# Seven block products for the last twelve weight chunks of a hybrid convolution and attention layer

## The chip, the cores and the metric

One core of a Trainium2 chip. The time is device microseconds of one launch. The engines are TensorE (PE, its weight loads PEld), VectorE (DVE), ScalarE (ACT), GpSimd (POOL, idle here) and SyncE (SP), whose queue issues nearly all transfers. Every engine takes its queue in order.

## What is computed

One layer over 512 tokens of width 1024 (and 256 context tokens), cut from the reference:

```python
h  = rmsnorm(x, pre_g) * (1 + sc) + sh              # sc, sh, gt = split(silu(c) @ w_mod + b_mod)
b_gate, c_gate, x_in, z_a, q, k, v, z_b, g_a, g_b = split(h @ w_in)      # ten blocks of 1024 columns
attn = neighbourhood_attention(rope(q), rope(k), v, k_ctx, v_ctx, rpb)   # 16 heads of 64
y_a = (silu(z_a) * b_gate * dwconv3(c_gate * x_in, conv_w, conv_b)) @ w_out_conv
y_b = (silu(z_b) * attn) @ w_out_attn
y   = (sigmoid(g_a) * y_a + sigmoid(g_b) * y_b) @ w_o
out = x + gt * rmsnorm(y, post_g)
```

All in fp32.

## The kernel before

**Products.** An fp32 operand is held as two fp32r tiles, H (a cast on ScalarE) and L (the remainder, a subtraction on VectorE); `split` (L67) makes both. A product is H·H + H·L + L·H, three matmuls for each 128 rows of depth. Activations stand with channels on the partitions and tokens along the free axis (`hx`, 8 tiles of 128 channels x 512 tokens).

**Weight chunks.** `w_in` and the two output projections are read in chunks of 1024 rows x 256 columns: two units of 128 columns. `Chunk` loads one as two raw halves of 512 KB (`raw`), and splits each half (128x1024 on ACT and on DVE) into a tile `w`. `Chunks` keeps one chunk ahead. `unit(w, i)` multiplies a unit with h: 24 matmuls of 512 columns (`step_T`, L115 to L117).

**Stages.** First x is normed, the modulation computed and the first three chunks multiplied, in an order written by hand (`manual_schedule`). Then four convolution groups and the modulated context; here `conv_out` (L191) writes its result to `u`, eight halves of four tiles in SBUF. Then attention: eight pairs of heads, for each head four blocks of 128 queries (64 score blocks in all): scores on PE, the addition of the bias with a minimum on DVE (L568), exp and scaling on ACT, transposes (L583) whose result is split into TH and TL, and the product with V (`gather`, L599). Between the blocks stand the chunks that `plan` names for each pair: queries and keys (`qk`), values (`v`), the later convolutions (`cx`, `bz`), gates of the attention (`zb`) and merge gates (`g`). The last gate `gate2(3)` follows, and the splits of u and attention into `us` and `as` (L696).

Then eight merges: `y_j` multiplies a chunk of output projections with `us` and `as`, is gated with `G[j]` and summed to the merged tile `m`; the merge gates g2 to g7 stand between y0 to y6, one after each. At last comes the product with `w_o`, which is done in seven block products already (L801).

The order within the stages that are not written by hand is the Tile framework's: its scheduler orders each engine's instructions by the data they need and by their place in the code, and pools' buffers decide which load can start.

Of the kernel before, what the change touches and what calls it, by code (L numbers as in the profile page):

```python
# [15 lines left out]
P = 128  # L16
D = 1024
# [10 lines left out]
def layer(ctx: ExitStack, tc, xp, ctxt, ctxT, cc, wmod, small, wfirst, win, wout, wo, rel, tab, out):  # L28
# [6 lines left out]
    pp = ctx.enter_context(tc.tile_pool(name="pp", bufs=1, space=bass.MemoryType.PSUM))  # L35

# [18 lines left out]
    def pairs(tag, n, dtype=F32R):  # L55
        t = [hp.tile([P, 2, n], dtype, name=f"{tag}{k}") for k in range(KT)]
        return t, ([x[:, 0] for x in t], [x[:, 1] for x in t])

    def halves(tag):
        t = [hp.tile([P, 2, S], F32, name=f"{tag}{i}") for i in range(4)]  # L60
        return [t[i // 2][:, i % 2] for i in range(KT)]


    _, hx = pairs("h", S)
    hcs, hc = pairs("hc", C)
# [11 lines left out]

    class Chunk:


        def __init__(self, src):
            self.raws = [wp.tile([P, 4, 256], F32, name="raw", bufs=2) for _ in range(2)]
            for i, raw in enumerate(self.raws):
                nc.sync.dma_start(raw, src[:, 4 * i:4 * i + 4])

        def split(self):
            both = wp.tile([P, KT, 2, 256], F32R, name="w", bufs=2)
            for i, raw in enumerate(self.raws):
                s = slice(4 * i, 4 * i + 4)
                split(both[:, s, 0], both[:, s, 1], raw)  # L90
            return both[:, :, 0], both[:, :, 1], both

    def load_chunk(src):
        return Chunk(src).split()

    class Chunks:
# [5 lines left out]
        def load(self, n):  # L102
            if n < len(self.srcs) and n not in self.ahead:
                self.ahead[n] = load_chunk(self.srcs[n])

        def __call__(self):
            self.load(self.n)
            self.n += 1
            self.load(self.n)
            return self.ahead[self.n - 1]  # L110

    def step_T(ps, w, u, m, k):
        (H, L, _), (mH, mL) = w, m
        cs = slice(u * P, (u + 1) * P)
        nc.tensor.matmul(ps, lhsT=H[:, k, cs], rhs=mH[k], start=k == 0, stop=False)  # L115
        nc.tensor.matmul(ps, lhsT=H[:, k, cs], rhs=mL[k], start=False, stop=False)  # L116
        nc.tensor.matmul(ps, lhsT=L[:, k, cs], rhs=mH[k], start=False, stop=k == KT - 1)  # L117
# [6 lines left out]
    def proj_N(ps, w, m, ts):  # L124

        (H, _, both), (mH, mL) = w, m
        for k in range(KT):
            nc.tensor.matmul(  # L128
                ps, lhsT=mH[k][:, ts], rhs=both[:, k].rearrange("p a c -> p (a c)"), start=k == 0, stop=False,
                skip_group_check=True,  # L130
            )
        for k in range(KT):
            nc.tensor.matmul(  # L133
                ps[:, :256], lhsT=mL[k][:, ts], rhs=H[:, k], start=False, stop=k == KT - 1, skip_group_check=True
            )

    def proj_c(ps, w, u):

        (H, L, _), cs = w, slice(u * P, (u + 1) * P)
        for k in range(KT):  # L140
            nc.tensor.matmul(  # L141
                ps, lhsT=H[:, k, cs], rhs=hcs[k].rearrange("p a c -> p (a c)"), start=k == 0, stop=False,
                skip_group_check=True,
            )
        for k in range(KT):
            nc.tensor.matmul(  # L146
                ps[:, :C], lhsT=L[:, k, cs], rhs=hc[0][k], start=False, stop=k == KT - 1, skip_group_check=True
            )
# [29 lines left out]
    order = [win[i] for i in range(8)] + [qk(0), vz(0, 0)]  # L178
    order += [where[n](i) for f in plan for n, i in f] + [vz(3, 1)]
    for j in range(KT):  # L180
        order += [wout[j]] + ([win[34 + j]] if j < 6 else [])
# [53 lines left out]
    with ExitStack() as p0:  # L235
# [36 lines left out]
        ones = const.tile([1, P], F32, name="ones")  # L272
# [6 lines left out]
        u = halves("u")  # L279
# [35 lines left out]
        with tc.manual_schedule(engines={E.PE, E.DVE, E.Activation, E.SP}):  # L315
# [74 lines left out]
            for k in range(KT):  # L390
# [15 lines left out]
                elif k == 5:  # L406
                    after = Chunk(order[3])
# [62 lines left out]
    attn = halves("a")  # L470
# [137 lines left out]
    def gate(p, w, i):  # L608
        psz = unit(w, i)
# [7 lines left out]
    def gate2(g):  # L617
        w = chunk()
        gate(2 * g, w, 0)
        yield  # L620
        gate(2 * g + 1, w, 1)
        yield
# [3 lines left out]
    def merge_gates(j):  # L626
        w = chunk()
        G[j] = []
        for i in range(2):
            n = 2 * j + i  # L630
            g = hp.tile([P, S], F32, name=f"g{n}", tag=f"hc{n % 8}")
            nc.scalar.activation(g, unit(w, i), AF.Tanh, scale=0.5)  # L632
            G[j].append(g)
            yield
# [13 lines left out]
    convs = {j: conv(j) for j in range(4, KT)}  # L648
# [53 lines left out]
    raws = [hp.tile([P, 2, S], F32, name=f"m{i}", tag=f"u{i}") for i in range(4)]  # L702
    m2 = [raws[i // 2][:, i % 2] for i in range(KT)]
# [7 lines left out]
    def block(name, pool, tags):  # L711
# [19 lines left out]
    A11, S3 = operand("A11", hp, ("a0", "a1")), operand("S3", hp, ("a2", "a3"))  # L731
    B11, B12 = block("B11", bp, ("B0", "B1")), block("B12", bp, ("B2", "B3"))
# [10 lines left out]
    for j in range(KT):  # L743
        w = chunk()
        g = G[j]
        for i in range(2):
# [3 lines left out]
            if j == 7 and i == 0:  # L750
                A2 = [bp.tile([P, 2, S], F32R, name=f"A2{k}", tag=f"us{k}") for k in range(4)]
                for k in range(3):
                    split(A2[k][:, 0], A2[k][:, 1], m2[k + 4])
        nc.vector.tensor_add(m2[j], g[0], g[1])
        if j < 4:
            split(A11[j // 2][:, 0, j % 2], A11[j // 2][:, 1, j % 2], m2[j][:, h0])
        if j == 1 or j == 3:
            q = j // 2
            x = cv.tile([P, S], F32, name="tb").rearrange("p (k c) -> p k c", k=2)
            nc.vector.tensor_sub(x, raws[q][:, :, h0], raws[q][:, :, h1])  # L760
            split(S3[q][:, 0], S3[q][:, 1], x)
        if j < 6:
            for _ in merge_gates(j + 2):
                pass
        if j == 3:
            load_block(B11, 0, 0)
            load_block(B12, 0, 1)
        if j == 4:
# [4 lines left out]
            for i in range(2):  # L773
# [6 lines left out]
                nc.scalar.copy(gpost[:, i * S:(i + 1) * S], ps)  # L780
        if j == 5:
            sums1(0)
            B22, B21, T2, T3 = (block(n, hp, (f"h{2 * i}", f"h{2 * i + 1}")) for i, n in enumerate(("B22", "B21", "T2", "T3")))
            load_block(B22, 1, 1)
            load_block(B21, 1, 0)
        if j == 6:
            nc.scalar.activation(const.tile([P, 1], F32, name="dummy2"), G[7][1][:, :1], AF.Sqrt, bias=eps, scale=0.0)
# [8 lines left out]
    def product(ps, a, w, start, t, cols=slice(0, S), out=None):  # L796
# [9 lines left out]
    def both(ps, a, w, start, then=lambda t: None):  # L806
        for t in range(2):
            product(ps[t], a, w, start, t)
            then(t)

    xr = [[hp.tile([P, S], F32, name=f"xr{t}{i}", tag=f"hc{2 * t + i}") for i in range(2)] for t in range(4)]
# [25 lines left out]
    def close(t, n, parts):  # L837
# [157 lines left out]
```

## Time and profile before

| | |
|---|---|
| median of 3 runs | 723.36 us (723.33 to 723.99) |
| the profiled execution's own time | 723.86 us |
| its span, first to last instruction | 722.1 us |
| granted TensorE clock | 0.999 |
| busy: PE, DVE, ACT | 711.1, 507.3, 392.8 us |
| read and written in HBM | 83.93 MB, 2.10 MB |

The profile is of the profiled execution, which is 0.5 us above the median. In the page's rows an operation stands by its line in the kernel, its engine, and its tiles, written out<-in. A line can be that of a helper: nearly all splits have the lines of `split` (L70 on ACT, L71 on DVE), so there the tile tells what it is. Matmuls overlap each other in their records; what one costs in a row of them is the distance of their starts.

### The profile page before, as it was taken

How to read it: one execution, taken by the hardware profiler on the slowest of the kernel's cores; microseconds unless marked ns; L12 is line 12 of the kernel's file. 1: busy time of each engine (PE TensorE's matmuls, PEld its weight loads, DVE VectorE, ACT ScalarE, POOL GpSimd, SP SyncE). 2: the span in 40 equal slices, each digit the busy share in tenths (PEclk: the TensorE clock that was granted, in tenths of full speed). 3: DMA queues.
4: the chain of work that ended last, by engine and by line, in shares of the span. 5: the costliest groups of instructions: out<-in, count | busy, mean ns of one | idle time of the engine just before them, and what ended most of it. 6: DMA issues, size and time to landing. Idle time of an engine off the chain costs nothing.

```text
span 722.1 us, 9274 instructions
## 1 busy us (share of the span) xinstructions
PE 711.1 (98%) x3476; PEld 596.9 (83%) x3476; DVE 507.3 (70%) x955; ACT 392.8 (54%) x706; POOL 0.7 (0%) x6
## 2 busy tenths in 40 slices
PE   7999999999999999999999999999999999999996
PEld 4888888888888888888888888888888888888885
DVE  6979999794887848758768678565763333343997
ACT  6576533674676755755657647555742223133573
POOL 0000000000000000000000000000000000000000
PEclk9999999999999999999999999999999999999999
DMA  8985883213122122122321222222442322424103
GB/s 340 405 325 189 312 266 116 89 62 113 59 74 74 59 87 74 59 73 74 99 93 44 74 89 72 74 80 95 130 138 83 116 87 89 145 91 171 59 1 117
DMA packets 26543, 86.63 MB, mean 120 GB/s; under 512 B 3073, under 2 KB 3329, under 8 KB 26498
## 3 DMA queue, kind: packets, MB, share of 16 engines
q1 hardware_dynamic: 26354, 85.90, 35.1%
q8 instruction: 27, 0.44, 0.3%
q14 instruction: 18, 0.15, 0.1%
q10 hardware_dynamic: 144, 0.13, 0.1%
HBM read 83.93 MB, written 2.10 MB: 119 GB/s over the span
## 4 chain that ended last, share of the span: by engine, by line
PE 96%; DVE 1%; DMA 1%; SPq 0%; ACT 0%; issue 0%; DVEq 0%; ACTq 0%
PE ps L116 21%; PE ps L117 21%; PE ps L115 21%; PE ps L128 6%; PE ps L801 5%; PE ps L599 4%; PE ps L583 4%; PE ps L133 3%; PE ps L552 3%; PE ps L141 2%; PE ps L307 2%; PE ps L311 2%; PE ps L308 2%; DMA fraw<-in_wfirst 1%; PE ps L561 1%; PE ps L146 1%
## 5 line engine op out<-in xcount | busy, mean ns | idle before, releaser
L115 PE MATMUL ps<-h,w 128*128 128x512 f32 x528 | 207.6, 393 | 0.0
L117 PE MATMUL ps<-h,w 128*128 128x512 f32 x528 | 205.7, 390 | 0.0
L116 PE MATMUL ps<-h,w 128*128 128x512 f32 x528 | 205.7, 390 | 0.0
L71 DVE TENSOR_TENSOR w<-raw,w 128x1024 fp32r<-128x1024 f32 x90 | 107.8, 1218 | 49.1 <-ACT w L70 48.9
L70 ACT CAST w<-raw 128x1024 fp32r<-128x1024 f32 x90 | 92.0, 1050 | 72.5 <-PE ps L117 64.6
L117 PEld LDWEIGHTS ps<-h,w 128*128 128x128 f32 x528 | 99.1, 188 | 20.7
L116 PEld LDWEIGHTS ps<-h,w 128*128 128x128 f32 x528 | 99.2, 188 | 20.2
L115 PEld LDWEIGHTS ps<-h,w 128*128 128x128 f32 x528 | 99.2, 188 | 20.1
L574 ACT ACTIVATE pt<-ps,m 128x512 f32<-128x512 f32 x64 | 44.1, 690 | 32.2 <-DVE m L568 31.8
L576 ACT ACTIVATE pt<-pt,z 128x512 f32<-128x512 f32 x64 | 46.7, 731 | 13.9 <-DVE z L575 13.9
L568 DVE CUSTOM_DVE_ANT_1 ps<-ps,bt 128x512 f32<-128x512 f32 x56 | 38.6, 699 | 19.0 <-PE ps L552 14.6
L71 DVE TENSOR_TENSOR TL<-ps,TH 128x512 fp32r<-128x512 f32 x64 | 43.1, 682 | 10.3 <-ACT TH L70 10.3
L747 DVE SCALAR_TENSOR_TENSOR g<-g,ps 128x512 f32<-128x512 f32 x16 | 11.0, 687 | 39.9 <-PE ps L117 39.9
L632 ACT ACTIVATE g<-ps 128x512 f32<-128x512 f32 x16 | 9.6, 598 | 54.1 <-PE ps L117 54.1
L70 ACT CAST TH<-ps 128x512 fp32r<-128x512 f32 x64 | 35.6, 589 | 3.6 <-PE ps L583 3.4
L583 PE MATMUL ps<-ident,pt 128*128 128x128 f32 x256 | 33.4, 273 | 0.2 <-DVE TL L71 0.2
L128 PE MATMUL ps<-w,h 128*128 128x512 f32 x128 | 32.5, 394 | 0.0
L583 PEld LDWEIGHTS ps<-ident,pt 128*128 128x128 f32 x256 | 29.2, 141 | 2.8 <-issue 0.6
L599 PE MATMUL ps<-TH,V 128*128 128x256 f32 (+1 forms) x96 | 28.5, 319 | 0.0
L517 ACT ACTIVATE qd<-ta 64x512 fp32r<-64x512 f32 x32 | 20.2, 631 | 14.2 <-DVE ta L491 11.3
L599 PE MATMUL ps<-TL,V 128*128 128x256 f32 (+1 forms) x96 | 27.7, 318 | 0.0
L128 PEld LDWEIGHTS ps<-w,h 128*128 128x128 f32 x128 | 23.1, 189 | 4.2
(192 smaller groups left out, 1169.6 us busy)
## 6 DMA issues: line engine op xcount, KB each, us to landing
raw<-in_win SPq DMA_DIRECT2D x74, 512.0 KB, 4.2
wm<-in_wmod SPq DMA_DIRECT2D x34, 512.0 KB, 7.1
raw<-in_wout SPq DMA_DIRECT2D x16, 512.0 KB, 4.6
bt<-in_rel SPq DMA_DIRECT2D x16, 256.0 KB, 2.6
B<-in_wo SPq DMA_DIRECT2D x8, 512.0 KB, 7.2
fraw<-in_wfirst SPq DMA_DIRECT2D x8, 384.0 KB, 8.7
x<-in_xp SPq DMA_DIRECT2D x4, 512.0 KB, 5.2
xr<-in_xp SPq DMA_DIRECT2D x8, 256.0 KB, 3.0
```

What stands on the lines that cost most here:

```text
L70: nc.scalar.copy(H, src)
L71: nc.vector.tensor_sub(L, src, H.bitcast(F32))
L115: nc.tensor.matmul(ps, lhsT=H[:, k, cs], rhs=mH[k], start=k == 0, stop=False)
L116: nc.tensor.matmul(ps, lhsT=H[:, k, cs], rhs=mL[k], start=False, stop=False)
L117: nc.tensor.matmul(ps, lhsT=L[:, k, cs], rhs=mH[k], start=False, stop=k == KT - 1)
L128: nc.tensor.matmul(ps, lhsT=mH[k][:, ts], rhs=both[:, k].rearrange("p a c -> p (a c)"), start=k == 0, stop=False, skip_group_check=True,)
L568: nc.vector.tensor_tensor_reduce(out=s3, in0=s3, in1=bt[:, e::4 - e][:, 0:2], scale=-1.0, scalar=3.0e38, op0=ALU.add, op1=ALU.min, accum_o ...
L574: nc.scalar.activation(pt, s, AF.Exp, bias=m, scale=-1.0, accum_out=z)
L576: nc.scalar.mul(pt, pt, z)
L583: nc.tensor.transpose(tp[:, c], pt[:, c * P:(c + 1) * P], ident)
L599: nc.tensor.matmul(o3[:, dst], lhsT=V[p][:, kt, h], rhs=src(t), start=n == 0 and t is TH, stop=n == len(work) - 1 and t is TL,)
L801: nc.tensor.matmul(out, lhsT=a(x, k, ts), rhs=w[y][k // 2][:, k % 2, cols], start=start and k + o == 0, stop=k == 3 and o == 2, skip_group ...
```

## The change

**Pairs.** Twelve chunks of w_in, those for which `paired` holds (zb2, zb3, the two chunks of convolution 7, and all eight g), are multiplied by `pair` instead of twice `unit`. A chunk W (1024 x 256) times h (1024 x 512) is seen as 2 x 2 blocks: depth in two halves, W's columns as its two units, and the tokens as two halves of 256. Winograd's form of Strassen's method takes seven block products (A11·B11, A12·B21, X1·T1, S2·T2, A22·T4, S3·T3, S4·B22), each 4 x 3 matmuls of 256 columns, so 84 in the place of 48 of 512. T1 to T4 are sums of the chunk's blocks, made on DVE in the raw tiles; each of the seven is split by itself (128x512). `first` prepares B11, B21, T1, T2 ahead, `second` T4, T3, B22 when the chunk's turn comes. The products are put together in the outputs by four copies on ACT and four combinations of 256 columns on DVE (L275, L283, L286).

**Block sums of h.** S2, S3, S4 and X1 (`block_sums`) are made once, in four steps, split, and kept in the tiles that held u and part of the attention.

**DRAM.** u goes to DRAM (`usc`, 8 x 256 KB) as soon as it is made, and the attention of the first two gates too (`asc`, 2 x 512 KB); both come back before the merges.

**Around it.** `w` becomes half tiles in four buffers, `raw` has three buffers for two. The merge order is written as the list `merge`: g2, g3, y0, g4, y1, g5, y2, g6, y3, g7, y4 to y7. A merge gate takes one tanh of 1024 elements. S3, A11 and the loads of all of w_o stand in the fifth merge, and x comes back in four loads.

The diff's core:

```diff
+    def first(self):
+        (b11, b12), (b21, b22) = self.b = [(r[:, :, :P], r[:, :, P:]) for r in self.raws]
+        t, sums = (wtile([P, 2, 2, 4, P]) for _ in range(2))
+        for x, b in ((t[:, 0], b11), (t[:, 1], b21)):
+            split(x[:, 0], x[:, 1], b)
+        nc.vector.tensor_add(b11, b11, b12)
+        split(sums[:, 0, 0], sums[:, 0, 1], b11)
+        nc.vector.tensor_add(b11, b11, b22)
+        split(sums[:, 1, 0], sums[:, 1, 1], b11)
+        nc.vector.tensor_add(b21, b21, b11)
+        nc.vector.tensor_add(b12, b12, b22)
+        self.B = {"B11": t[:, 0], "B21": t[:, 1], "T1": sums[:, 0], "T2": sums[:, 1]}
+        return self
+
+    def second(self):
+        t, last = (wtile([P, 2, 2, 4, P]) for _ in range(2))
+        for n, x, b in (("T4", t[:, 0], self.b[1][0]), ("T3", t[:, 1], self.b[0][1]), ("B22", last[:, 0], self.b[1][1])):
+            split(x[:, 0], x[:, 1], b)
+            self.B[n] = x
...
+def product(ps, act, w, start):
+    for k in range(4):
+        for x, y, o in ((0, 0, 0), (0, 1, 1), (1, 0, 2)):
+            nc.tensor.matmul(ps, lhsT=w[:, x, k], rhs=act[y][k], start=start and k + o == 0, ...)
+
+def pair(c1, c2):
+    w = chunk().B
+    a, b, e = (pj()[:, :256] for _ in range(3))
+    first, second = slice(0, 256), slice(256, S)
+    product(a, A11, w["B11"], True)
+    nc.scalar.copy(c1[:, first], a)
+    product(b, A12, w["B21"], True)
+    product(e, blocks_h["X1"], w["T1"], True)
+    nc.scalar.copy(c2[:, second], e)
+    product(a, blocks_h["S2"], w["T2"], False)
+    nc.scalar.copy(c2[:, first], a)
+    nc.vector.tensor_add(c1[:, first], c1[:, first], b)
+    chunk.more()
+    yield
+    product(b, A22, w["T4"], True)
+    product(a, blocks_h["S3"], w["T3"], False)
+    nc.scalar.copy(c1[:, second], a)
+    product(e, blocks_h["S4"], w["B22"], False)
+    for cols, x in ((second, c1[:, second]), (first, e)):
+        nc.vector.scalar_tensor_tensor(out=c2[:, cols], in0=c2[:, cols], scalar=-1.0, in1=x, op0=ALU.mult, op1=ALU.subtract)
+    nc.vector.tensor_add(c1[:, second], c1[:, second], b)
...
-        nc.vector.tensor_mul(u[j], y, z)
+        nc.vector.tensor_mul(y, y, z)
+        nc.sync.dma_start(usc[j], y)
...
+    reloaded = [bp.tile([P, S], F32, name=f"ur{k}", tag=f"as{k}") for k in range(KT)]
+    early = [cv.tile([P, S], F32, name=("ta", "tb")[k % 2]) for k in range(4)]
+    for k in range(KT):
+        nc.sync.dma_start(reloaded[k], usc[k])
+    for k in range(4):
+        nc.sync.dma_start(early[k], asc[k // 2][:, k % 2])
```

**Where the instructions stand after the attention, on VectorE.** Before, between the gates of the last attention tiles (L612, L613) and the first merge (L747); `us` and `as` are the split u and attention, `w` a chunk's halves:

```order
L612 SCALAR_TENSOR_TENSOR tb_4930<-tb_4930,ps_4905 128x512
L71 TENSOR_TENSOR as4_4966<-a2_1025,as4_4966 128x512
L613 SCALAR_TENSOR_TENSOR a3_1026<-a3_1026,tb_4930 128x512
L71 TENSOR_TENSOR as5_4967<-a2_1025,as5_4967 128x512
L71 TENSOR_TENSOR as6_4968<-a3_1026,as6_4968 128x512
L71 TENSOR_TENSOR as7_4969<-a3_1026,as7_4969 128x512
L71 TENSOR_TENSOR w_5002<-raw_4998,w_5002 128x4x256
L71 TENSOR_TENSOR w_5002<-raw_4999,w_5002 128x4x256
L747 SCALAR_TENSOR_TENSOR g0_4629<-g0_4629,ps_5007 128x512
```

After, from zb3's last combinations (L283, L286) on; L722 and L723 are the gates, `ur` the u that came back:

```order
L283 SCALAR_TENSOR_TENSOR tc_5283<-tc_5283,ps_5294 128x256
L286 TENSOR_TENSOR tc_5282<-tc_5282,ps_5293 128x256
L68 TENSOR_TENSOR us1_5444<-ur1_5418,us1_5444 128x512
L68 TENSOR_TENSOR us2_5447<-ur2_5419,us2_5447 128x512
L722 SCALAR_TENSOR_TENSOR tb_5405<-tb_5405,tc_5282 128x512
L722 SCALAR_TENSOR_TENSOR tb_5409<-tb_5409,tc_5283 128x512
L723 SCALAR_TENSOR_TENSOR at6_4509<-at6_4509,tb_5405 128x512
L723 SCALAR_TENSOR_TENSOR at6_4509<-at6_4509,tb_5409 128x512
L68 TENSOR_TENSOR us3_5450<-ur3_5420,us3_5450 128x512
```

Behind these stand us4 to us7 and as0 to as5, and then:

```order
L68 TENSOR_TENSOR as6_5483<-at6_4509,as6_5483 128x512
L68 TENSOR_TENSOR as7_5486<-at6_4509,as7_5486 128x512
L68 TENSOR_TENSOR w_5490<-raw_5348,w_5490 128x512
L68 TENSOR_TENSOR w_5490<-raw_5347,w_5490 128x512
L68 TENSOR_TENSOR w_5491<-raw_5348,w_5491 128x512
L275 TENSOR_TENSOR g2_5489<-g2_5489,ps_5499 128x256
L68 TENSOR_TENSOR w_5557<-raw_5553,w_5557 128x512
```

All splits of u but the first, and all of attention, stand between zb3's last combination and the three splits of g2's second half (T4, T3, B22; `w_5490` and `w_5491`). Before, no chunk stood behind them but the first of the merges.

**On TensorE at the same place.** Before, zb3's second unit (a unit reads h) is followed by y0, which reads `us` (three matmuls for each depth of 128):

```order
L115 MATMUL ps_4905<-h7_87,w_4751 128x512
L116 MATMUL ps_4905<-h7_87,w_4751 128x512
L117 MATMUL ps_4905<-h7_87,w_4751 128x512
L115 MATMUL ps_5007<-us0_4938,w_4871 128x512
L116 MATMUL ps_5007<-us0_4938,w_4871 128x512
L117 MATMUL ps_5007<-us0_4938,w_4871 128x512
```

After (`S2`, `S3`, `S4`, as `S20` and `S40`, are tiles with two block sums of h, x3 three matmuls):

```order
L258 MATMUL ps_5498<-S22_3700,w_5352 128x256 x3
L258 MATMUL ps_5498<-S23_3816,w_5352 128x256 x3
L258 MATMUL ps_5500<-S40_3411,w_5491 128x256 x2
L258 MATMUL ps_5621<-h0_82,w_5557 128x256 x2
L258 MATMUL ps_5498<-S20_3408,w_5490 128x256 x3
L258 MATMUL ps_5498<-S21_3543,w_5490 128x256 x3
L258 MATMUL ps_5498<-S22_3700,w_5490 128x256 x3
L258 MATMUL ps_5498<-S23_3816,w_5490 128x256 x2
L258 MATMUL ps_5499<-h4_86,w_5490 128x256 x3
```

Here g2 stands right behind zb3, g3 behind g2, and y0 behind both; the row with `S20_3408,w_5490` is g2's product with T3, after two matmuls of its last product and two of g3's first.

More of the change, by code (lines that the diff above doesn't have):

```diff
@@ L53, in layer @@
     gains = const.tile([P, KT], F32, name="gains")
[L55 to L65, printed above, removed]
+    th = [hp.tile([P, 2, S], F32R, name=f"h{k}") for k in range(KT)]
+    hx = [t[:, 0] for t in th], [t[:, 1] for t in th]
+    thc = [hp.tile([P, 2, 2, C], F32R, name=f"hc{i}") for i in range(4)]
+    hcs = [thc[k // 2][:, k % 2] for k in range(KT)]
+    hc = [t[:, 0] for t in hcs], [t[:, 1] for t in hcs]
+    usc = [dr.tile([P, S], F32, name=f"usc{j}") for j in range(KT)]
+    asc = [dr.tile([P, 2, S], F32, name=f"asc{g}") for g in range(2)]
     def split(H, L, src, scale=None):
@@ L76, in split, with wtile @@
             )
+    def wtile(shape):
+        return wp.tile(shape, F32R, name="w", bufs=4)
     class Chunk:
         def __init__(self, src):
-            self.raws = [wp.tile([P, 4, 256], F32, name="raw", bufs=2) for _ in range(2)]
+            self.raws = [wp.tile([P, 4, 256], F32, name="raw", bufs=3) for _ in range(2)]
             for i, raw in enumerate(self.raws):
@@ L86, in split @@
         def split(self):
[L87 to L94, printed above, removed]
+            t = [wtile([P, 4, 2, 256]) for _ in range(2)]
+            for x, raw in zip(t, self.raws):
+                split(x[:, :, 0], x[:, :, 1], raw)
+            k = range(KT)
+            return tuple([t[i // 4][:, i % 4, y] for i in k] for y in range(2)) + ([t[i // 4][:, i % 4] for i in k],)
+        def first(self):
[16 more added lines that the diff above has]
+                self.B[n] = x
     class Chunks:
@@ L103, in load @@
             if n < len(self.srcs) and n not in self.ahead:
-                self.ahead[n] = load_chunk(self.srcs[n])
+                src, paired = self.srcs[n]
+                self.ahead[n] = Chunk(src).first() if paired else Chunk(src).split()
         def __call__(self):
@@ L108, in __call__, with more @@
             self.n += 1
+            w = self.ahead[self.n - 1]
+            if isinstance(w, Chunk):
+                w.second()
+            else:
+                self.load(self.n)
+            return w
+        def more(self):
             self.load(self.n)
-            return self.ahead[self.n - 1]
     def step_T(ps, w, u, m, k):
@@ L177, in layer, with paired @@
     }
[L178 to L181, printed above, removed]
+    def paired(n, i):
+        return n == "g" or n == "zb" and i > 1 or n in ("cx", "bz") and i > 6
+    order = [(win[i], False) for i in range(8)] + [(qk(0), False), (vz(0, 0), False)]
+    order += [(where[n](i), paired(n, i)) for f in plan for n, i in f] + [(vz(3, 1), paired("zb", 3))]
+    merge = ["g2", "g3", "y0", "g4", "y1", "g5", "y2", "g6", "y3", "g7", "y4", "y5", "y6", "y7"]
+    order += [(win[32 + int(m[1])], True) if m[0] == "g" else (wout[int(m[1])], False) for m in merge]
     chunk = Chunks(order)
@@ L212, in conv_out, with block, both_units, conv_pairs @@
         nc.vector.tensor_mul(z, z, psb)
-        nc.vector.tensor_mul(u[j], y, z)
+        nc.vector.tensor_mul(y, y, z)
+        nc.sync.dma_start(usc[j], y)
+    def block(i, j):
+        h = hx
+        ks, ts = slice(4 * i, 4 * i + 4), slice(256 * j, 256 * j + 256)
+        return [[x[:, ts] for x in y[ks]] for y in h]
+    A11, A12, A22 = block(0, 0), block(1, 0), block(1, 1)
+    blocks_h = {}
+    def product(ps, act, w, start):
+        for k in range(4):
+            for x, y, o in ((0, 0, 0), (0, 1, 1), (1, 0, 2)):
+                nc.tensor.matmul(
+                    ps, lhsT=w[:, x, k], rhs=act[y][k], start=start and k + o == 0, stop=k == 3 and o == 2,
+                    skip_group_check=True,
+                )
+    def pair(c1, c2):
[17 more added lines that the diff above has]
+        for cols, x in ((second, c1[:, second]), (first, e)):
+            nc.vector.scalar_tensor_tensor(
+                out=c2[:, cols], in0=c2[:, cols], scalar=-1.0, in1=x, op0=ALU.mult, op1=ALU.subtract
+            )
+        nc.vector.tensor_add(c1[:, second], c1[:, second], b)
+    def both_units():
+        return [cv.tile([P, S], F32, name="tc") for _ in range(2)]
+    def conv_pairs(j):
+        c, x = both_units()
+        yield from pair(c, x)
+        cs = cv.tile([P, S], F32, name="cs", bufs=1)
+        nc.vector.tensor_mul(cs, c, x)
+        yield
+        b, z = both_units()
+        yield from pair(b, z)
+        conv_out(j, cs, b, z)
+        yield
     def conv(j):
@@ L406, in layer @@
                 elif k == 5:
-                    after = Chunk(order[3])
+                    after = Chunk(order[3][0])
                 steps(k)
@@ L617, in gate2 @@
     def gate2(g):
[L618 to L621, printed above, removed]
+        if paired("zb", g):
+            z = both_units()
+            yield from pair(*z)
+            for i in range(2):
+                gate(2 * g + i, z[i])
+        else:
+            w = chunk()
+            gate(2 * g, unit(w, 0))
+            yield
+            gate(2 * g + 1, unit(w, 1))
+        if g < 2:
+            nc.sync.dma_start(asc[g], attn[2 * g, "both"])
         yield
@@ L626, in merge_gates @@
     def merge_gates(j):
[L627 to L634, printed above, removed]
+        G[j] = hp.tile([P, 2, S], F32, name=f"g{j}", tag=f"hc{j % 4}")
+        yield from pair(G[j][:, 0], G[j][:, 1])
+        nc.scalar.activation(G[j], G[j], AF.Tanh, scale=0.5)
+        yield
     def chain(*gs):
@@ L647, in layer @@
             pass
-    convs = {j: conv(j) for j in range(4, KT)}
+    convs = {j: conv_pairs(j) if paired("cx", j) else conv(j) for j in range(4, KT)}
     fill = []
@@ L662, in layer @@
     T = None
+    sums = block_sums()
     done = 0
@@ L668, in layer @@
             total, done = sum(n for _, n in fill[p]), 0
+        if i in (36, 38, 41, 43):
+            next(sums)
         upto = -(-total * (slot + 1) // 8)
@@ L744, in layer @@
         w = chunk()
-        g = G[j]
+        g = [G[j][:, i] for i in range(2)]
+        if j in (4, 6):
+            raws[j // 2] = G[j]
+        m2 = raws[j // 2][:, j % 2]
         for i in range(2):
@@ L794, in layer, with tokens @@
             total(T4, T2, B21)
-    def product(ps, a, w, start, t, cols=slice(0, S), out=None):
+    def tokens(ps, a, w, start, t, cols=slice(0, S), out=None):
         ts = slice(t * P, (t + 1) * P)
@@ L807, in both @@
         for t in range(2):
-            product(ps[t], a, w, start, t)
+            tokens(ps[t], a, w, start, t)
             then(t)
-    xr = [[hp.tile([P, S], F32, name=f"xr{t}{i}", tag=f"hc{2 * t + i}") for i in range(2)] for t in range(4)]
+    xr = [hp.tile([P, D], F32, name=f"xr{t}", tag=f"hc{(1, 3, 0, 2)[t]}") for t in range(4)]
     ys = [bp.tile([P, D], F32, name=f"ys{t}", tag=f"as{2 + t}") for t in range(4)]
```

109 lines of the change are left out of this document (64 added, 45 removed).

## The prediction

> **What bounds the kernel now.** I read the page's first part, then the waits of TensorE, then busy times by stage, then single stretches of the timeline.
>
> From the page (busy us, share, instructions; a group's busy us and mean ns; the KB and us to landing of a load):
>
> ```profile
> PE 711.1 (98%) x3476; PEld 596.9 (83%) x3476; DVE 507.3 (70%) x955; ACT 392.8 (54%) x706; POOL 0.7 (0%) x6
> L70 ACT CAST w<-raw 128x1024 fp32r<-128x1024 f32 x90 | 92.0, 1050 | 72.5 <-PE ps L117 64.6
> raw<-in_win SPq DMA_DIRECT2D x74, 512.0 KB, 4.2
> bt<-in_rel SPq DMA_DIRECT2D x16, 256.0 KB, 2.6
> ```
>
> All that TensorE waited for (us in total, times, longest):
>
> ```profile
> PE ps L355 <- ACT crow L327: 3.3, 1, 3.3
> PE ps L307 <- ACT h L70: 1.2, 1, 1.2
> PE ps L583 <- DVE TL L71: 0.2, 1, 0.2
> ```
>
> After the startup PE never waits: the time is the number of its matmuls by their spacing. The stretches below (length, then PE, PEld, DVE, ACT, POOL busy, clock, DMA share, GB/s) tell how much room VectorE has beside it:
>
> ```profile
> 0.00:54.00 54.00, 49.33 (x209) 37.62 (x210) 44.38 (x81) 35.49 (x50) 0.70 (x6) 1.00 0.93 357
> 54.00:72.00 18.00, 18.00 (x81) 14.90 (x80) 17.46 (x30) 11.00 (x19) 0.00 (x0) 1.00 0.56 191
> 72.00:90.00 18.00, 18.00 (x81) 14.92 (x80) 17.61 (x32) 10.12 (x19) 0.00 (x0) 1.00 0.88 309
> 117.00:361.77 244.77, 244.60 (x1293) 209.66 (x1292) 186.02 (x403) 156.21 (x311) 0.00 (x0) 1.00 0.24 79
> 436.73:504.31 67.58, 67.58 (x341) 57.25 (x340) 43.52 (x94) 41.22 (x75) 0.00 (x0) 1.00 0.27 85
> 504.31:540.00 35.69, 35.69 (x170) 29.66 (x169) 25.97 (x39) 20.44 (x35) 0.00 (x0) 1.00 0.39 127
> 580.00:620.00 40.00, 40.00 (x178) 33.10 (x178) 14.21 (x17) 10.34 (x14) 0.00 (x0) 1.00 0.33 106
> 677.00:722.00 45.00, 38.91 (x183) 32.50 (x182) 39.80 (x64) 26.41 (x47) 0.00 (x0) 0.98 0.16 59
> ```
>
> 436.73 and 504.31 are the score reductions of blocks 51 and 63, so this row is most of the last two head pairs. DVE has 24 us free there, 26 of 40 in the merges, and next to none in the convolutions and the last product. The changed chunks stand in the last pairs and the merges.
>
> **Matmuls.** From the timeline (start, duration), first PE, then VectorE and ScalarE:
>
> ```profile
> 145.85 0.39 PE L115 MATMUL ps<-h,w 128*128 128x512 f32 x1
> ...
> 148.57 0.39 PE L115 MATMUL ps<-h,w 128*128 128x512 f32 x1
> ...
> 149.72 1.03 PE L583 MATMUL ps<-ident,pt 128*128 128x128 f32 x8
> 150.51 2.10 PE L141 MATMUL ps<-hc,w 128*128 128x512 f32 x8
> 152.45 1.11 PE L146 MATMUL ps<-hc,w 128*128 128x256 f32 x8
> 153.40 0.40 PE L552 MATMUL ps<-ks,qd 128*128 128x512 f32 x1
> ...
> 710.15 5.75 PE L801 MATMUL ps<-w,A 128*128 128x512 f32 x36
> ```
>
> ```profile
> 71.81 0.76 DVE L71 TENSOR_TENSOR hc<-ctT,hc 128x256 fp32r<-128x256 f32 x2
> ...
> 522.74 2.49 DVE L71 TENSOR_TENSOR as<-a,as 128x512 fp32r<-128x512 f32 x4
> ...
> 527.19 1.89 DVE L71 TENSOR_TENSOR as<-a,as 128x512 fp32r<-128x512 f32 x3
> 528.99 2.36 DVE L71 TENSOR_TENSOR w<-raw,w 128x1024 fp32r<-128x1024 f32 x2
> ```
>
> ```profile
> 521.11 3.74 ACT L70 CAST as<-a 128x512 fp32r<-128x512 f32 x7
> ```
>
> Twelve matmuls of 512 columns take 148.57 - 145.85 = 2.72 us, 0.2267 each; eight of 256 take 0.95, 0.1188 each; eight of 128 take 0.79, 0.099 each. A chunk as two units is 48 of 512, 10.88 us; as seven products 84 of 256, 9.98. Twelve chunks: **-10.8 us**. The stretch of 36 (12 of 512, 24 of 256) less the 0.16 by which its last record outlasts its spacing gives 0.1196 for 256, and -10.0; the eight of L141 give 0.2425 for 512, which would be -19.9. I take -10.8, since the other pitches hold a change of group. Only a 256 pitch above 0.1295 would make the change lose on PE itself.
>
> The Trainium skill, "TensorE: Matmul & The Clock Gate", section "Back-to-back issue gap", gives a sustained spacing of 81 ns at 128 columns and 131 ns at 512, so that half the columns cost much more than half the time; on a straight line 256 would be about 98 ns (an estimate from that page), 84 of them 8.2 us against 6.3 for 48 of 512, and the sum would be +23 us. The trace does not agree (99, 119 and 227 ns), and the measurement decides.
>
> **VectorE and ScalarE per paired chunk.** Spacing on DVE: 512 elements 0.60, 1024 1.14, 256 0.34; ACT casts 0.52 at 512. A chunk had two splits, 2 x 1.14 = 2.3 us of DVE. Now: seven splits and four weight sums of 512, 6.6, and four combinations of 256, 1.4: 8.0, that is +5.7 on DVE, and at most +3.6 on ACT (seven casts and four copies at 0.52 for two casts of 1.05). Against 9.98 us of PE that is harmless alone, and in the merges, where PE spends 20.9 us on a y and a g chunk and DVE about 12.1 (8.0, a y chunk's two splits, three operations of 512). In pairs 6 and 7 the scores need DVE too. Between the reductions of blocks 51 and 63 the changed program has 48 more operations of 512, 17 more of 256, ten fewer of 1024 and eight fewer small copies: +28.9 +5.8 -11.4 -1.2 = +22.1 on 42.1 (the row's 43.5 without the 0.09 that a lone operation's record outlasts its spacing), so 64 us. PE there has 384 matmuls of 256, 35 of 512 and 48 of 128: 58.3. From block 51 to the end of the paired zb3, DVE 81.1 (97 of 512, 25 of 256, 13 reductions and what belongs to them), PE 82.4. VectorE is as full as TensorE.
>
> **After zb3 (its end is Z).** DVE takes its queue in order. Behind zb3's last combination, which needs zb3's last matmul, stand two operations of 256 and then 21 of 512 up to g2's T3: eight splits of u, four gates, the eight of attention, g2's T4 and then T3. That is 0.7 + 12.6 + 0.3 for the start = 13.6. PE needs the T3 remainder after 54 matmuls of 256, at Z + 6.4. It waits **7.2 us**. Before, the splits of u and attention stood behind the gates too, but PE came to each at 0.68 us a step (three matmuls) and DVE at 0.60, so it was never short. The block of g2 now stands in between. T3's split is also what frees the raw buffer of g3's second half: Z + 13.6 + 4.2 (the landing) = 17.8, cast and split to 19.1, the sums built on it and g3's last seven splits to about 25.4, with PE at g3's second half 1.7 us before. Then y0 starts near Z + 29 where PE's own work is 20.4: **+9.0** (8 to 10) for the jam. The list's loads come in time: u's are issued at the end of the last attention product, some 65 matmuls (7.7 us) ahead of Z, at 2.6 us each; two attention tiles reload after the gates, near Z + 4, land by Z + 7 and are split from Z + 8 on. A jam is shorter only if Z itself comes late, which costs the same.
>
> **Gaps in the 82 us of full DVE.** Every wait of DVE there (for a cast, for a raw half that lands 4.2 us after T3's split, for a PSUM bank) now moves PE. Not shown before. Ends: 0, if 81.1 fits 82.4; by the share that DVE reaches in 677 to 722, 39.80 of 45, it needs 91.7, +9.3. The convolutions reach 17.5 of 18 (97%): 83.3, +0.9. The score chain crosses engines oftener than convolutions, yet has two blocks of lead; I take 95%, 85.4, **+3**.
>
> **The rest.** Block sums of h: four times (four of 512, four of 256) = 15 us of DVE, 4 of ACT. The first group stands in the startup and the first convolution, the others among head pair 0's projections and the first scores, needed only at zb2. Cover there:
>
> ```profile
> 40.31 0.69 DVE L71 TENSOR_TENSOR h<-m,h 128x512 fp32r<-128x512 f32 x1 [0.36 <-ACT h L70]
> ...
> 44.93 0.69 DVE L71 TENSOR_TENSOR h<-m,h 128x512 fp32r<-128x512 f32 x1 [1.70 <-ACT h L70]
> ```
>
> These gaps and 59 free us from 117 on. 0; if the cover fails, the first group's 3.7 in the full convolutions. More DVE work can't gain. Stores of u and two attention pairs (3 MB) and their reloads stand on SP's queue, each store ahead of raw loads and waiting for its tile. A raw half lands in 4.2 us and is asked for one chunk (10 us) ahead, DMA share 0.24: 0, at worst +1. The third raw buffer is in the g3 step above. One tanh of 1024 for two of 512, x in four loads for eight, A11, S3 and the w_o loads moved to the fifth merge: DVE has 26 of 40 us free there and SP four loads more in a row; 0, +-1, the cover being that 26. The tail's operations stay, and DVE is full there as before.
>
> Sum against the profiled execution (723.86, of which the span is 722.1): -10.8 + 9.0 + 3 + 0 = +1.2, 725.1. The median of the runs is 0.5 lower, so **724.6**.
>
> **Rivals.**
> A. The pairs jam throughout (slower): from block 51 on DVE needs 64 us where PE needs 58, and its gaps go by the tail's share, +9.3: -10.8 + 9 + 9.3 = +7.5, 730.9. It decides from a DVE share under 0.92. For: no row before shows scores beside so many splits. Against: reductions lead by two blocks.
> B. The saving arrives (faster): g2's first half and g3's start hide the splits, because DVE comes to Z ahead, or ACT's casts fall so that the splits run earlier: -10.8 + 0 to 3, 712.6 to 715.6. Against: the queue's order, and a gate that needs zb3's product.
> C. The jam stands, DVE has no gaps, as in the convolutions (+0.9 or less) and the jam is 8: -10.8 + 8 + 0.5 = -2.3, 721.1 (719 to 721.9). It decides from a DVE share of about 0.98.
> D. The change does nothing on PE, since 256 columns cost 0.1295 among switches of weights: 0 on PE, +12 from DVE, 735. Against: the 36-run above, which switches each time.
>
> **Chances.** Forecast 0.55 (722 to 728), A 0.15, B 0.10, C 0.18, D 0.02. About 0.2%, 1.4 us, is what can be told from no change. Of the forecast's 0.55, half lies within it (gaps under 3.2 us) and half above. Faster: B, C and a little of the forecast, 0.30; same 0.27; slower, A, D and 0.26 of the forecast, 0.43. The likeliest case's own range is 722 to 728; the full range leaves out most of B and the upper part of A and D: 717 to 731.
>
> **What the profile after would show.** PE busy near 700. In its waits a line for the product of the blocks, released by the weights' remainder on DVE, 7 us long once just after the attention and a second of 1 to 2. DVE's share from the last pairs to y0 at 95% or more, with gaps toward ACT's casts and raw loads. No new wait before zb2, none in the merges from y0 on. Wrong would be: no wait after zb3 (then B), waits of several us in each chunk of pairs 6 and 7 (A), a 256 spacing over 0.12 (D), or waits in the convolutions.

## The result, and the profile after

The changed kernel takes **728.63 us** (median of 4 runs, 727.38 to 729.10) against 723.59 for the kernel before (723.33 to 723.99): ratio 1.0066, 95% interval 1.0051 to 1.0081, so 5.0 us slower, outside what could pass for no change. The forecast was 724.6, slower, with a range of 717 to 731. The profiled execution took 729.1 us, with a span of 727.3.

From the page of the changed kernel (busy us), and from its list of transfers the reloads of u (KB each, median us from issue to landing):

```profile
PE 706.9 (97%) x3908; PEld 613.1 (84%) x3908; DVE 593.9 (82%) x1141; ACT 437.1 (60%) x811; POOL 0.7 (0%) x6
ur<-usc SPq DMA_DIRECT2D x8, 256.0 KB, 6.9
```

TensorE is busy only 4.2 us less than before, though its products were to save 10.8, and it waits more. What it waited for from the last pairs on (us in total, times, longest):

```profile
PE ps L258 <- ACT g L269: 5.2, 1, 5.2
PE ps L258 <- DVE tc L283: 1.7, 1, 1.7
PE ps L691 <- DVE TL L68: 0.9, 1, 0.9
PE ps L710 <- DVE TL L68: 0.6, 1, 0.6
PE ps L691 <- ACT pt L684: 0.6, 1, 0.6
PE ps L258 <- DVE tc L286: 0.3, 1, 0.3
PE ps L258 <- ACT tc L269: 0.3, 1, 0.3
PE ps L258 <- ACT g L280: 0.2, 1, 0.2
```

Before, TensorE did not wait at all in this part. L258 is the paired products. The first two lines stand behind zb3: the wait of 1.7 us begins at 524.74, the long one at 530.26. The others stand in pairs 6 and 7. Stages (length, then busy of PE, PEld, DVE, ACT, POOL, granted clock, DMA share, GB/s); the first row is of the kernel before, the others are of the changed one:

```profile
440.00:520.00 80.00, 80.00 (x403) 67.51 (x402) 50.42 (x104) 49.01 (x88) 0.00 (x0) 1.00 0.26 84
```

```profile
72.00:90.00 18.00, 18.00 (x81) 14.90 (x80) 17.55 (x34) 9.54 (x18) 0.00 (x0) 1.00 0.91 316
440.00:520.00 80.00, 77.15 (x605) 73.76 (x604) 75.09 (x160) 61.20 (x127) 0.00 (x0) 1.00 0.27 90
530.20:535.40 5.20, 0.06 (x1) 0.00 (x0) 5.20 (x10) 5.08 (x12) 0.00 (x0) 0.91 0.33 101
535.40:538.60 3.20, 3.11 (x14) 3.11 (x15) 3.20 (x6) 0.97 (x4) 0.00 (x0) 0.50 0.00 0
538.60:541.50 2.90, 2.90 (x16) 2.90 (x15) 2.90 (x7) 0.23 (x1) 0.00 (x0) 0.53 0.36 93
541.50:545.00 3.50, 3.50 (x32) 3.50 (x31) 2.42 (x10) 1.74 (x4) 0.00 (x0) 1.00 0.64 229
```

The convolutions are as they were. In the last pairs VectorE went from 50.4 to 75.1 of 80 us (94%). In the long wait VectorE and ScalarE were both full, and behind it TensorE ran on half its clock for 6 us. The chain that ended last, from the reload of u up to g3's last 36 matmuls (550.37), goes through none of TensorE's own work (start, us, what):

```profile
516.67 6.44 DMA ur<-usc
...
523.14 0.63 ACT us L67
...
526.68 1.20 DVE us L68 x2
527.88 1.21 DVE tb L722 x2
...
530.29 2.21 DVE us L68 x4
...
533.22 2.02 DVE as L68 x4
...
535.63 2.49 DVE as L68 x4
538.12 1.22 DVE w L68 x2
...
539.39 4.68 DMA raw<-in_win
...
544.09 0.69 DVE raw L106
```

Behind the reload that is the list of the prediction: u's splits, the gates, attention's splits, T4 and T3 of g2, then the load into the raw buffer that T3 frees, then g3's sums.

### The profile page after: what moved, and what is told of

The parts are those of the page before. It is cut to its first block, busy times and chain, and to the rows that moved or that the text cites. A ratio compares the mean times of both kernels' runs of the same rounds, so it can differ in the third digit from the quotient of the medians.

```text
span 727.3 us, 10524 instructions
## 1 busy us (share of the span) xinstructions
PE 706.9 (97%) x3908; PEld 613.1 (84%) x3908; DVE 593.9 (82%) x1141; ACT 437.1 (60%) x811; POOL 0.7 (0%) x6
## 4 chain that ended last, share of the span: by engine, by line
PE 81%; DVE 9%; DMA 5%; ACT 2%; issue 1%; SPq 1%; DVEq 0%; ACTq 0%
PE ps L145 15%; PE ps L144 14%; PE ps L143 14%; PE ps L258 7%; PE ps L156 6%; PE ps L926 5%; PE ps L710 3%; PE ps L161 3%; PE ps L691 3%; DMA raw<-in_win 3%; PE ps L660 2%; DVE w L68 2%; PE ps L393 2%; PE ps L397 2%; PE ps L394 2%; PE ps L169 2%
## 5 line engine op out<-in xcount | busy, mean ns | idle before, releaser
L67 ACT CAST w<-raw 128x512 fp32r<-128x512 f32 (+1 forms) x150 | 119.6, 809 | 89.3 <-PE ps L145 39.0
L68 DVE TENSOR_TENSOR w<-raw,w 128x512 fp32r<-128x512 f32 (+1 forms) x150 | 135.7, 919 | 37.6 <-ACT w L67 36.9
L143 PE MATMUL ps<-h,w 128*128 128x512 f32 x336 | 132.3, 394 | 0.0
L145 PE MATMUL ps<-h,w 128*128 128x512 f32 x336 | 130.9, 390 | 0.0
L144 PE MATMUL ps<-h,w 128*128 128x512 f32 x336 | 130.9, 390 | 0.0
L258 PE MATMUL ps<-S,w 128*128 128x256 f32 x576 | 76.6, 289 | 5.6 <-ACT g L269 5.2
L258 PEld LDWEIGHTS ps<-S,w 128*128 128x128 f32 x576 | 73.5, 198 | 6.6 <-ACT g L269 5.4
L145 PEld LDWEIGHTS ps<-h,w 128*128 128x128 f32 x336 | 63.1, 188 | 13.2
L144 PEld LDWEIGHTS ps<-h,w 128*128 128x128 f32 x336 | 63.1, 188 | 12.8
L143 PEld LDWEIGHTS ps<-h,w 128*128 128x128 f32 x336 | 63.1, 188 | 12.9
L258 PE MATMUL ps<-h,w 128*128 128x256 f32 x432 | 57.9, 285 | 2.2 <-DVE tc L283 1.7
L258 PEld LDWEIGHTS ps<-h,w 128*128 128x128 f32 x432 | 54.5, 192 | 3.6 <-DVE tc L283 1.9
```

The costliest lines, as they stand in the source:

```text
L67: nc.scalar.copy(H, src)
L68: nc.vector.tensor_sub(L, src, H.bitcast(F32))
L143: nc.tensor.matmul(ps, lhsT=H[k][:, cs], rhs=mH[k], start=k == 0, stop=False)
L144: nc.tensor.matmul(ps, lhsT=H[k][:, cs], rhs=mL[k], start=False, stop=False)
L145: nc.tensor.matmul(ps, lhsT=L[k][:, cs], rhs=mH[k], start=False, stop=k == KT - 1)
L258: nc.tensor.matmul(ps, lhsT=w[:, x, k], rhs=act[y][k], start=start and k + o == 0, stop=k == 3 and o == 2, skip_group_check=True,)
```

## Experiments

Times are medians; the ratio to the kernel before has its 95% interval. Each was timed beside runs of the kernel before on the same chip, whose medians were 723.62 to 723.99 us.

### The splits behind g2 and g3

```diff
+    for j in (2, 3):
+        for _ in merge_gates(j):
+            pass
     for n, srcs in (("u", reloaded), ("a", early + [attn[k] for k in range(4, KT)])):
         ...
-    for j in (2, 3):
-        for _ in merge_gates(j):
-            pass
```

> Edit: the sixteen splits of u and attention stand in the code behind g2 and g3 instead of ahead of them; the work is the same. Theory J (the jam): the sixteen casts on ScalarE hold back the copy that g2's fourth product waits for (5.2 us in the changed kernel's waits), and TensorE then runs 27 matmuls at about 0.22 us instead of 0.12 (2.7 us); both go, the wait of 1.7 us on zb3's combination stays: 728.6 - 8 = 720.6 (719 to 722.5), granted clock back to 0.999. Rival V (the list must be done anyway: VectorE and ScalarE are full, so the wait only moves to g3 or to y0): 726 or more, with a wait of 4 to 5 us at y0. Rival P (the loss is in the paired chunks themselves, in pairs 6 and 7): no change, 728.

Measured **721.07 us** (0.9967, 0.9954 to 0.9979): 7.6 us less than the changed kernel, and 2.8 us faster than before the change (723.91 beside it). Theory J said 720.6. Of the waits behind zb3 only the first is left:

```profile
PE ps L258 <- DVE tc L283: 1.6, 1, 1.6
```

The granted clock over the span is 0.998 (0.994 in the changed kernel). So most of the loss behind zb3 was not the amount of the list but its place. Rivals V and P fall as the whole explanation.

### Only the merge gates paired

```diff
-        return n == "g" or n == "zb" and i > 1 or n in ("cx", "bz") and i > 6
+        return n == "g"
```

> Edit: only the eight merge gates are multiplied in seven products; zb2, zb3 and the two chunks of convolution 7 go back to two units. Theory J: the four chunks in the attention gain 4 x 0.7 to 0.9 on TensorE and cost about 3 us of waits in pairs 6 and 7 (0.9, 0.6, 0.6 and five of 0.2 to 0.3), so taking them back changes little: 727.5 to 729.5, and the wait of about 5 us after zb3 stays. Rival P (the paired chunks beside scores are what loses): 724 or less.

Measured **721.77 us** (0.9973, 0.9963 to 0.9984). Theory J's 728 was a miss; rival P is right here: the four paired chunks beside the scores lose more than they gain. Of the waits in pairs 6 and 7 none is left, and the long one is shorter too: the casts of the reloaded u begin at 518.2 us here, 4.7 us ahead of zb3's end, where in the changed kernel they begin 0.9 us ahead of it, so ScalarE and VectorE have less left to do:

```profile
PE ps L258 <- ACT g L269: 2.9, 1, 2.9
```

So there are two losses. The late splits take away one; taking the four chunks back takes away the other and shortens the first.

### No chunk paired

```diff
-        return n == "g" or n == "zb" and i > 1 or n in ("cx", "bz") and i > 6
+        return False
...
-        yield from pair(G[j][:, 0], G[j][:, 1])
-        nc.scalar.activation(G[j], G[j], AF.Tanh, scale=0.5)
-        yield
+        w = chunk()
+        for i in range(2):
+            nc.scalar.activation(G[j][:, i], unit(w, i), AF.Tanh, scale=0.5)
+            yield
```

> Edit: no chunk is multiplied in seven products; the block sums of h are still made and not used, and the way of u and attention by DRAM, the buffers, the merge order and the moves of the tail stay. It measures all that stands around the products. My prediction counted 0 for it outside the jam: 723.5 to 724.5, and with the sixteen splits ahead of g3's weights one wait of up to 3 us more, 726.5. Rival R (the way by DRAM and the block sums cost several us in themselves): 728 or more, with waits in the convolutions or the startup.

Measured **724.19 us** (1.0004, 0.9996 to 1.0013): no difference from before. Block sums, the way by DRAM, buffers, merge order and the moves of the tail cost nothing by themselves, as the prediction had it. Rival R is out.

### u not loaded back

```diff
-    reloaded = [bp.tile([P, S], F32, name=f"ur{k}", tag=f"as{k}") for k in range(KT)]
+    reloaded = [hx[0][k].bitcast(F32) for k in range(KT)]
...
-    for k in range(KT):
-        nc.sync.dma_start(reloaded[k], usc[k])
```

> Edit: u is still stored but not loaded back; the splits of u read tiles of h instead (the output is then another one; work and counts of the splits are the same). Theory J with its own first part: the cast of the first reloaded tile held ScalarE 2.2 us and VectorE 1.4, behind it zb3's last combination, for which TensorE waited 1.7 us: that wait goes, 728.6 - 1.7 = 726.9 (726 to 727.5), the 5 us wait stays. Rival (the reload is hidden, the 1.7 us is VectorE's own backlog): 728.6. Rival W: with the first casts earlier the whole list comes forward by 2 us and the long wait is shorter too, 724 to 726.

Measured **728.76 us** (1.0064, 1.0051 to 1.0077), the same as the changed kernel, so the expected 1.7 us did not come. The wait for L283 is gone, and the long one appears in two parts:

```profile
PE ps L258 <- DVE w L68: 4.0, 1, 4.0
PE ps L258 <- ACT g L269: 1.8, 1, 1.8
```

The 4.0 us is g2's T3 on VectorE, the very wait that the prediction had; in the changed kernel the longer wait for ScalarE's copy (L269), behind its casts, and the slow matmuls after it took up this time. T3 is now there at 537.1 us, about 2.2 us sooner than by the chain above (539.3); 0.5 of this is an earlier end of zb3. Why little of it is seen in the time, the chain (start, us, what) and two stages show:

```profile
537.13 16.03 PE ps L258 x114
```

```profile
532.00:537.00 5.00, 1.08 (x6) 0.79 (x4) 4.82 (x9) 0.73 (x2) 0.00 (x0) 0.50 0.00 0
537.00:543.20 6.20, 6.07 (x33) 6.07 (x34) 5.29 (x16) 2.03 (x4) 0.00 (x0) 0.61 0.51 173
```

TensorE has half its clock here too (0.50, 0.61), and now it is itself the chain: 114 matmuls take 16.03 us, 0.141 each, where 0.12 would be 13.7. That costs 2.4 us, about what T3 had gained. In the changed kernel the same slow matmuls lie beside the 4.68 us load.

### TensorE kept busy in the wait

```diff
         product(e, blocks_h["X1"], w["T1"], True)
+        for _ in range(44 if chunk.n == 10 + sum(map(len, plan)) + 2 else 0):
+            nc.tensor.matmul(spare, lhsT=hx[0][0][:, :P], rhs=hx[0][0][:, :256], start=True, stop=True)
```

> Edit: in the changed kernel, 44 matmuls of 256 columns into an unused bank stand where TensorE waits 5.2 us for the copy of g2's first product; nothing else moves on VectorE. Theory K (the slow matmuls after the wait, 27 at 0.22 us, come from the idle time and cost their 2.6 us): granted clock 0.999 and 726.0. Theory J (VectorE's list sets when g2's T3 is there, at 539.2 us by the trace, whatever TensorE's rate): the clock is back, but TensorE then waits about 2 us at T3: 728.6 - 0 to 1.0. Rival: the clock stays low, the cause is not the idle time: 728.6 with 0.994.

Measured **727.74 us** (1.0048, 1.0035 to 1.0062), 0.9 less than the changed kernel, with the intervals of the two overlapping: theory J. The timeline of TensorE (the row of 44 is the filling) and one stage:

```profile
530.07 5.44 PE L273 MATMUL ps<-h 128*128 128x256 f32 x44
536.15 1.94 PE L258 MATMUL ps<-S,w 128*128 128x256 f32 x14 [0.65 <-ACT g L269]
...
539.35 1.34 PE L258 MATMUL ps<-S,w 128*128 128x256 f32 x9 [0.53 <-DVE w L68]
```

```profile
530.00:540.00 10.00, 8.82 (x69) 8.22 (x69) 10.00 (x18) 6.55 (x14) 0.00 (x0) 1.00 0.16 54
```

The clock stays at 1.00 and 14 matmuls take 1.8 us, not 3.2; so the low clock came from the idle time. But TensorE then waits for T3, which is there at 539.3 as before. So the low clock cost the changed kernel no more than about 0.9 us; VectorE's list sets the time here. Theory K falls: it had asked for 726.0.

### y0 first in the merge order

```diff
-    merge = ["g2", "g3", "y0", "g4", "y1", "g5", "y2", "g6", "y3", "g7", "y4", "y5", "y6", "y7"]
+    merge = ["y0", "g2", "y1", "g3", "y2", "g4", "y3", "g5", "g6", "g7", "y4", "y5", "y6", "y7"]
...
```

(The loops that start the merge gates are moved to match; up to g5 the order is that of the kernel before.)

> Edit: all twelve chunks paired, the splits where the changed kernel has them, but the merge order begins with y0 as before the change (y0 g2 y1 g3 y2 g4 y3 g5 g6 g7 y4 to y7). Theory J (the order g2 g3 y0 puts a chunk's second half and the next chunk's weights behind sixteen splits that nobody needs yet): y0 takes the splits as they come (three matmuls of 512, 0.68 us, for each split of 0.60), the waits after zb3 shrink from 7.3 us to about 3 (the reload and the gates stay ahead of the rest), the clock stays up: 728.6 - 5 = 723.5 (721.5 to 725). Rival V (VectorE's total after zb3 is what counts, wherever it stands): 727 or more. In the version with late splits the same list cost nothing, 721.1, so 721 would say that the order alone did it.

Measured **723.85 us** (1.0001, 0.9993 to 1.0010), 4.8 us less than the changed kernel, as theory J had it. TensorE reads the splits as VectorE makes them:

```profile
PE ps L143 <- DVE tc L283: 1.9, 1, 1.9
...
PE ps L144 <- DVE as L68: 0.4, 1, 0.4
```

It isn't at 721, as the version with late splits is. Small waits at y0 and g2 (0.3 to 0.4 us each) are a part of these 2.8 us; the rest was not followed up.

### The load on VectorE beside the scores

```diff
+            def split(H, L, src):
+                nc.scalar.copy(H, src)
+                if not self.light:
+                    nc.vector.tensor_sub(L, src, H.bitcast(F32))
...
-                    ps, lhsT=w[:, x, k], rhs=act[y][k], ...
+                    ps, lhsT=w[:, 0 if low else x, k], rhs=act[y][k], ...
```

(`light` holds for the six paired chunks of the attention; with the splits behind g2 and g3.)

> Edit: late splits, and the six paired chunks of the attention (zb2, cx7, bz7, g0, g1, zb3) leave out the seven remainders L on VectorE (the products use H in their place; casts, sums, loads and matmuls stay): 4.2 us of VectorE less per chunk. Theory P-DVE (VectorE's load beside the scores makes the waits in pairs 6 and 7): the stretch from 440 to 512, which took 5 us more than its matmuls, comes back to about 1, and zb3's wait of 1.6 shrinks: 721.1 - 4.5 = 716.6 (715.5 to 718). Rival P-ACT or P-DMA (the casts, or the raw halves that VectorE waited 3.8 us for, set the pace): 720 to 721.5.

Measured **715.53 us** (0.9887, 0.9873 to 0.9900), 5.5 us below the version with late splits; forecast 4.5. Its waits in this part, and two quarters of the stage of pairs 6 and 7:

```profile
PE ps L267 <- ACT tc L278: 0.3, 1, 0.3
...
PE ps L267 <- DVE tc L292: 0.2, 1, 0.2
```

```profile
460.00:480.00 20.00, 20.00 (x162) 19.52 (x161) 15.09 (x35) 16.49 (x35) 0.00 (x0) 1.00 0.24 80
480.00:500.00 20.00, 20.00 (x161) 19.35 (x160) 13.79 (x33) 16.95 (x35) 0.00 (x0) 1.00 0.40 133
```

With the casts and loads in place and 4.2 us of VectorE fewer per chunk, the waits for TL and exp are gone, and of the 1.6 us behind zb3 0.2 is left; this last is a part of the 5.5. VectorE's load is the cause, not ScalarE's, which is no lower (16.5 and 17.0 of 20 us in these rows, where the changed kernel had 61.2 of 80 in its stage).

### Both cures together, and with zb3

```diff
-        return n == "g" or n == "zb" and i > 1 or n in ("cx", "bz") and i > 6
+        return n == "g"
...
+    for j in (2, 3):
+        for _ in merge_gates(j):
+            pass
     for n, srcs in (("u", reloaded), ("a", early + [attn[k] for k in range(4, KT)])):
```

> Edit: only the eight merge gates in seven products, and the splits of u and attention behind g2 and g3 (the two edits that gained most, together). Theory J+P (two separate losses: waits in pairs 6 and 7 from VectorE's load beside the scores, and the list of splits after zb3): in the version with g alone only a wait of 2.9 us is left, and it goes: 721.8 - 2.9 = 718.9 (718 to 719.8), no new wait of TensorE over 0.5 us. Rival V: the list returns as a wait at y0, 721 or more.

Measured **717.16 us** (0.9912, 0.9898 to 0.9925): 6.5 us faster than before, and the best version that leaves nothing out. TensorE waits here only at the start, for `crow`, `h` and `x`, and once for 0.2 us in the attention, as it does in the version with no chunk paired:

```profile
PE ps L441 <- ACT crow L413: 3.4, 1, 3.4
PE ps L393 <- ACT h L67: 1.2, 1, 1.2
PE ps L473 <- ACT x L437: 0.2, 1, 0.2
PE ps L691 <- ACT ks L636: 0.2, 1, 0.2
```

Eight chunks gave 6.5 us, 0.81 each; the forecast of 718.9 was 1.7 too high: it had taken off the listed 2.9 us alone. Two of the eight, g0 and g1, stand beside the scores of the last pair: by themselves they cost no wait there.

With zb3 as well:

```diff
-        return n == "g"
+        return n == "g" or n == "zb" and i > 2
```

> Edit: as the version before it, with zb3 paired too. A paired chunk measured 10.07 us undisturbed against 10.94 as two units, so the product gains 0.87; theory J+P: zb3 stands beside the last scores and ahead of the gates, and its combination waits behind the first reloaded tile (1.6 us in the version with late splits), so 718.9 - 0.9 + 1.6 to 2.0 = 719.7 (718.8 to 720.5). Rival: the gain arrives, 718.0.

Measured **717.16 us** (0.9909, 0.9896 to 0.9923), better than the expected 719.7 and no better than the version without zb3: the 0.9 us that zb3's products save do not reach the time, and the reload did not cost the 1.6 either. Which small waits eat it was not settled.

## Why the prediction was right, and where it was off

**The mechanism held; the sign had little behind it.** The forecast of +1.2 was smaller than the 1.4 us that it called no change, and 728.6 lies above the likeliest case's 722 to 728, so the number is in the range by the range's width. The mechanism is what the runs bear out. The prediction said that the products' saving would be lost to a list of splits behind zb3 and to a full VectorE in the last pairs, and these two are where the time went: late splits take away the first, lighter chunks the second, and without pairs nothing is left to explain. Rival A, a jam in every chunk, was to show in a VectorE share under 0.92; it was 0.94.

**Products: -10.8, measured about -9.8.** A paired chunk beside nothing, in the merges of the version with late splits (timeline):

```profile
577.68 3.04 PE L258 MATMUL ps<-h,w 128*128 128x256 f32 x24
...
587.75 0.40 PE L143 MATMUL ps<-us,w 128*128 128x512 f32 x1
```

The second row is the first matmul behind the chunk, so its 84 take 587.75 - 577.68 = 10.07 us, 0.120 each, against 10.88: 0.81 a chunk, the same as the eight merge gates gave. It was the second of the two prices from the rows, 0.1196 (-10.0), not the first. The spacing that the Trainium skill, "TensorE: Matmul & The Clock Gate", section "Back-to-back issue gap", gives (81 ns at 128 columns, 131 at 512), by which the sum would have been +23 us, is not what these matmuls do.

**The jam: +9.0, measured about +10.2.** The start of y0 (it reads `us`) in the changed kernel:

```profile
549.67 0.40 PE L143 MATMUL ps<-us,w 128*128 128x512 f32 x1
...
552.14 2.80 PE L258 MATMUL ps<-S,w 128*128 128x256 f32 x22
```

and in the version with late splits:

```profile
545.26 0.40 PE L143 MATMUL ps<-us,w 128*128 128x512 f32 x1
```

In the first, two matmuls of y0 stand ahead of g3's last 36, which end at 552.14 + 22 x 0.12 = 554.8, so y0 starts as if at 554.3: 9.1 us later. The version with late splits had come to zb3's end 0.6 sooner, and both have the first wait of 1.7: 9.1 - 0.6 + 1.7 = 10.2. The step "the list's loads come in time" failed: each of u's eight loads was taken at 2.6 us, but they landed 6.9 us after issue (median), and u's first split held up zb3's combinations. T3 came 15.3 us after zb3's end (524.0), not 13.6; without the reload it came 13.6 after it (537.1 against 523.5), as forecast. (The forecast's 21 operations are right, but its list names eight splits of u where seven stand.) And the long wait showed at another place, the copy of g2's first product on ScalarE, one step ahead of T3: I had counted VectorE's list alone, while ScalarE's queue, casts above all, held that copy until 535.1. The runs without the reload and with the filling show T3 close behind.

**Gaps in pairs 6 and 7: +3, measured about +4.3.** The first of the two rows is a score matmul ahead of all paired chunks, the second stands at zb3's end; before the change:

```profile
439.44 0.40 PE L552 MATMUL ps<-ks,qd 128*128 128x512 f32 x1
...
524.30 0.39 PE L115 MATMUL ps<-us,w 128*128 128x512 f32 x1
```

and after it, where 24 of the 30 matmuls are zb3's last:

```profile
439.54 0.40 PE L660 MATMUL ps<-ks,qd 128*128 128x512 f32 x1
...
520.98 3.76 PE L258 MATMUL ps<-S,w 128*128 128x256 f32 x30
```

The stretch took 84.9 us before, and 520.98 + 24 x 0.12 - 439.54 = 84.3 after. Its six paired chunks were to save 6 x 0.81 = 4.9 and saved 0.6, so the gaps took 4.3. The guess of a VectorE share of 95% was near (75.09 of 80, 94%). The six listed waits are 2.9 us together; a wait's record starts only where the record of the matmul ahead ends, 0.16 us later than its spacing, so with 0.16 for each they are 3.9. The 5.5 us that lighter chunks gave are near 4.3 and the 1.4 of the wait behind zb3 that went with them.

**The rest: 0, measured 0** (no chunk paired, 724.19 against 723.91).

-9.8 + 10.2 + 4.3 = +4.7, where the profiled executions differ by 729.1 - 723.86 = 5.2; the 0.5 between was not followed up. The forecast's +1.2 came from sizes that were all a little too kind: 1.0, 1.2 and 1.3.

## What to carry to other kernels

Cheaper matmuls that need more work on another engine pay only where that engine has room: the same edit gave 0.81 us a chunk in the merges, and beside the scores with two chunks paired, but lost there with six. Before changing the order of phases, look at what the in-order queues of the helping engines will hold between its halves; here sixteen splits that nobody needed for 20 us stood ahead of three that were needed at once, and moving them in the code by a few lines was worth 7.6 us. Here the engine's list of known length gave a better forecast (9.0 for 10.2) than its share of busy time (3 for 4.3), but count every queue with a list of its own, ScalarE's as well as VectorE's.

## What the chip showed that I had not expected

After the 5.2 us wait the granted clock was 0.50 for about 6 us, and 27 matmuls of 256 columns came at 0.21 to 0.23 us. The clock fell before the wait was over: the row from 530.2 to 535.4 has 0.91, which is 0.9 us at half, so it fell at about 534.5, some 4.2 us into the wait. After a wait of 2.9 us it did not fall (the version with only the merge gates paired, 29 matmuls in 3.7 us at 1.00):

```profile
530.30:534.00 3.70, 3.70 (x29) 3.51 (x29) 3.70 (x8) 1.11 (x3) 0.00 (x0) 1.00 0.19 53
```

Filling the wait with matmuls kept it at 1.00. But the length of one wait does not decide it. Without the reload the clock fell behind a wait of only 1.8 us:

```profile
530.06 2.18 PE L258 MATMUL ps<-S,w 128*128 128x256 f32 x14 [1.83 <-ACT g L269]
```

```profile
530.00:532.00 2.00, 1.94 (x14) 1.95 (x15) 2.00 (x5) 1.57 (x5) 0.00 (x0) 0.89 0.56 215
```

The 0.89 is about 0.4 us at half clock, so it fell near 531.6, while TensorE was at work and 1.5 us ahead of the second wait (4.0 us, from 533.1 on). The Trainium skill, "TensorE: Matmul & The Clock Gate", section "Part 1: The HAM clock gate (the 'warmup' mystery)", states half rate after an idle window of about 3.4 us; the run with the 5.2 us wait agrees, the fall behind 1.8 us does not follow from it, and its cause stays open here. A removed wait can so be worth less than its length, as the run without the reload showed: most of its 2.2 us went into slow matmuls.
